# A hybrid RG-LRU and SSD encoder step on one core: TensorE's order in the SSD stage written out by hand

## The chip, the cores and the metric

The kernel runs on one core of one Trainium2 chip. The metric is the device time of one execution in microseconds (us), the median of three runs. The profile is of one more execution of the same program, with a time and a span of its own.

## What is computed

One layer of a streaming encoder is applied to a prompt of 1024 tokens and to a sample of 32 tokens, both 1024 wide. All inputs are fp32. Cut to what matters here:

```python
mod = silu(c) @ w_ada + b_ada
shift, scale, gate = split(mod, 3)
h = rmsnorm(x, norm_g) * (1 + scale) + shift
lru_x, lru_g, xbc, z, dt_raw = split(h @ w_in)        # widths 1024, 1024, 1536, 1024, 16
# RG-LRU group: causal conv of width 4, gates, a scan over time, times silu(lru_g)
# SSD group, 16 heads of 64, 2 groups of B and C, state 128:
xs, B, C = split(silu(causal_conv(xbc)))
dt = softplus(dt_raw + dt_bias); dA = -exp(a_log) * dt
y = ssd_scan(xs * dt, dA, B, C, state) + d * xs        # within a chunk, and from chunk to chunk
y_ssd = grouped_rmsnorm(y * silu(z))
out = x + gate * (concat(y_lru, y_ssd) @ w_out);  y_out = rmsnorm(out, final_norm_g)
```

The new convolution rows and the new states are outputs as well.

## The kernel before, in words

Features lie on the 128 partitions and tokens on the free axis. Prompt and sample share one row of 1060 columns (`TW`): 1024 of the prompt, four of padding, 32 of the sample. The scan works in eight chunks of 128 tokens, and a ninth of the 32 sample tokens.

**Projection in units.** `w_in` is cut into units of 128 output columns. A unit's weights come by one DMA of 512 KB into `wraw` (`fetch_unit`, L96), ScalarE rounds them to `whi` (L101) and VectorE makes the rest `wlo` (L103), with three buffers of each. A unit is then 72 products on TensorE in three blocks of columns: block 2 (290 columns, with two shift columns), block 0 and block 1 (384 each). Each block takes eight times L236, L237, L238 into a PSUM tile `pj`. `pj` tiles have the tag "main" (four PSUM buffers). `shift_bias` (`sb`, L248, VectorE) and `evacuate` (L255, ScalarE) bring a unit to SBUF.

**Everything else on TensorE** in the SSD stage is short fp32 products into PSUM tiles with the tag "g", which are four buffers for all of them. One step of the stage handles one of eight pairs of heads, `j`:

- `ssd_tokens` (L643): nine transposes `xsT` (L652) of the tile `xs`, in three PSUM tiles; VectorE multiplies each into `xw` and `xdt` (L654).
- `ssd_states` (L658): nine products `dS` (L668) in three tiles; VectorE carries the state from chunk to chunk in 16 small instructions (L677).
- `ssd_diag` (L683): 18 products `yd` (L693) with the two decay matrices `M`; VectorE adds them with the skip term into `y` (L696).
- `ssd_off` (L700): eight products `yo` (L708) in three tiles of 384, 512 and 32 columns; VectorE multiplies each by `E` in place (L711), then adds it to `y` (L712). Only the add frees the tile's PSUM buffer.
- `ssd_decay` (L628) prepares the next step's `M` and `E`. SyncE's queue loads the two `M` tiles from `dA_d` in DRAM (L635) and `E` from `E_d` (L631), VectorE scans each `M` (L636), ScalarE takes the exponential (L639), and VectorE masks it with `CBm` (L640). `M` has two buffers, so the loads for step j+1 wait until the `yd` products of step j have read both.
- `gate_row` (L746): a 512 KB unit of `w_ada` and eight products `ada_s` (L120) of 128 columns, then `gate_column` (L750): one product `ada_c` (L127). One unit of the gate for each step.
- `ssd_x` (L754) makes `xs` by the convolution of a projected unit: one ScalarE instruction (L501), three on VectorE (L503), then silu on ScalarE. `ssd_z` and `ssd_gate` (L720) multiply `y` by silu of the z unit.

A step projects two units, x of the next step and z of its own. Once, at j = 4, `group_rstd` adds four products `gs` (L737).

**Ahead of the steps** lie four preparations: `b_post` for B (transposes `bT`, L599), `dt_chain` (a polynomial for softplus on VectorE, some fifty small instructions, then the two products `cs`, L553, and the transposes `dtT`, L570, whose copies go to DRAM as `dA_d` and `E_d` by 18 small DMAs on SyncE's queue, L575 and L576), and `c_post` for C (its convolution, then the products `cb`, L611, which are masked into `CBm`, L615). The units projected there are 27 (C of group 1) and 16 (x of step 0).

**What sets the order.** The start of the kernel is written out by hand for all engines (L313). From L464 on the framework's scheduler orders the instructions of every engine by its own estimate of when they are ready; the program's text gives only the dependences. Each engine takes its instructions strictly in the order that the scheduler has fixed. In the LRU stage that follows, ScalarE's order is by hand again.

Of the kernel before, what the change touches and what calls it, by code (L numbers as in the profile page):

```python
# [16 lines left out]
KT = 8  # L17
# [12 lines left out]
P_NG, P_BADA, P_LCW, P_LCB = 0, 8, 32, 64  # L30
# [33 lines left out]
def encoder_step(ctx: ExitStack, tc: tile.TileContext, a, o):  # L64
# [19 lines left out]
    def pc(base, i=0, n=1):  # L84
        return par[:, base + i:base + i + n]
# [20 lines left out]
    def load_unit(src):  # L106
        return split_unit(fetch_unit(src))
# [8 lines left out]
    def ada_unit(raw, n=1):  # L116
        ps = pbank([128, n * 128], "ada_s")
        for kk in range(KT):
            q = slice(32 * (kk % 4), 32 * (kk % 4) + 32)
            nc.tensor.matmul(ps[q, :], lhsT=sc[:, kk, :], rhs=raw[:, :, kk, :] if n > 1 else raw[:, kk, :],  # L120
                             start=(kk < 4), stop=(kk >= 4))
# [421 lines left out]
    def dt_chain():  # L543
        buf = tw.tile([128, TW], F32, name="dtbuf", tag="y", bufs=1)
        flat = [t.rearrange("p c h -> p (c h)") for t in (dt_tm, w_tm, dtv)]
        softplus(buf, flat[0], flat[2], 144)
        nega = buf[:, 0:16]
        nc.scalar.activation(nega, pc(P_ALOG, 0, 16), AF.Exp)
        nc.vector.tensor_scalar(nega, nega, -1.0, None, op0=OP.mult)
        dA = buf[:, 144:288]  # L550
        nc.vector.tensor_mul(dA.rearrange("p (c h) -> p c h", h=16), dt_tm, nega[:, None, :].to_broadcast([128, 9, 16]))
        ps = pbank([128, 2, 144], "cs")
        nc.tensor.matmul(ps[:, 0, :], lhsT=ge, rhs=dA, start=True, stop=True)  # L553
        nc.tensor.matmul(ps[:, 1, :], lhsT=ones[:, 0:128], rhs=dA, start=True, stop=True)
        Ee = buf[:, 288:432]
        cs = buf[:, 432:576]
        nc.vector.tensor_copy(cs, ps[:, 0, :])
        nc.scalar.activation(Ee, cs, AF.Exp)
        nc.vector.tensor_sub(cs, ps[:, 1, :], cs)
        nc.scalar.activation(cs, cs, AF.Exp)  # L560
        nc.vector.tensor_mul(flat[1], cs, flat[0])
        nc.gpsimd.memset(dec_bc, 0.0)
        nc.scalar.activation(dec_bc[:, 1:8, :].rearrange("p c h -> p (c h)"), ps[:, 1, 16:128], AF.Exp)
        nc.scalar.activation(dec_bc[:, 9, :], ps[:, 1, 128:144], AF.Exp)
        rows = tw.tile([128, TW], F32, name="dtrows", tag="E", bufs=1)
        nc.gpsimd.memset(rows[:, 0:328], 0.0)
        for i, (t, dst) in enumerate(((dA, dA_d), (Ee, E_d))):
            o0 = 164 * i
            pt = pbank([128, 160], "dtT2")
            nc.tensor.transpose(pt[:, 0:128], t[:, 0:128], ident)  # L570
            nc.tensor.transpose(pt[0:16, 128:160], t[0:32, 128:144], ident[0:32, 0:32])
            nc.vector.tensor_copy(rows[:, o0:o0 + 128], pt[:, 0:128])
            nc.vector.tensor_copy(rows[0:16, o0 + 132:o0 + 164], pt[0:16, 128:160])
            for c in range(NCH):
                dma(dst[:, c * 128:(c + 1) * 128], rows[c * 16:(c + 1) * 16, o0:o0 + 128])  # L575
# [25 lines left out]

    def c_post(g, raw):
        u = ssd_conv(raw, 10 + g)
        nc.scalar.activation(CT[:, g, :], u, AF.Silu)
        for cs_ in (range(0, 4), range(4, 8), range(8, 9)):
            n = len(cs_)
            L = chunk_cols(cs_[0])[1]
            pt = pbank([128, n, L], "cb")
            for i, c in enumerate(cs_):
                c0, L = chunk_cols(c)  # L610
                nc.tensor.matmul(pt[0:L, i, :], lhsT=BT[g][:, c0:c0 + L], rhs=CT[:, g, c0:c0 + L],  # L611
                                 start=True, stop=True)
# [4 lines left out]
    b_post(0, raws[0])
    with tc.issue_after(last[0].ins):
        banks = project(load_unit(a["w_in"][27]))
    b_post(1, raws[1])  # L620
    dt_chain()
    c_post(0, raws[2])
    c_post(1, ssd_raw(banks, 11))
# [119 lines left out]

    gate_rows = {}

    def gate_row(k):  # L746
        gate_rows[k] = wpool.tile([128, 128], F32, name="ada_row", tag="ada_row", bufs=2)
        nc.vector.tensor_copy(gate_rows[k], ada_unit(fetch_unit(a["w_ada"][16 + k])))

    def gate_column(k):  # L750
        pcol = ada_columns(gate_rows.pop(k), 1)
        nc.vector.tensor_scalar(gate[:, k, :], pcol[:, 0, :], pc(P_BADA, 16 + k), None, op0=OP.add)

    def ssd_x(j, raw):  # L754
        u = ssd_conv(raw, j)
        nc.scalar.activation(u, u, AF.Silu)
# [6 lines left out]
    with tc.issue_after(last[0].ins):
        xs = ssd_x(0, ssd_raw(project(load_unit(a["w_in"][16])), 0))
        gate_row(0)
    xdt, xw = ssd_tokens(0, xs)
    Ms, E = ssd_decay(0)
    stt = ssd_states(0, xw)
    for j in range(8):
        y = ssd_diag(j, xs, xdt, Ms)  # L770
        wx = load_unit(a["w_in"][17 + j if j < 7 else 0])
        banks = {}
        begin(wx, banks, 2)
        ssd_off(j, y, stt, E)
        banks = project(wx, (2, 0, 1), banks)
        if j < 7:
            Ms, E = ssd_decay(j + 1)
        if j < 7:
            xs = ssd_x(j + 1, ssd_raw(banks, j + 1))
        else:  # L780
            bx = lru_raw(banks, 0)
        wz = load_unit(a["w_in"][28 + j])
        banks = {}
        begin(wz, banks, 2)
        if j == 4:
            group_rstd(0)
        begin(wz, banks, 0)
        gate_column(j)
        if j < 7:
            xdt, xw = ssd_tokens(j + 1, xs)  # L790
        begin(wz, banks, 1)
        zs = ssd_z(banks)
        if j < 7:
            gate_row(j + 1)
            stt = ssd_states(j + 1, xw)
        ssd_gate(j, y, zs)
# [321 lines left out]
```

## Time and profile before

| | |
|---|---|
| median of 3 runs | 766.57 us (766.02 to 767.29) |
| profiled execution | 765.56 us, span 763.8 us |
| TensorE busy | 748.8 us, 98% of the span |
| VectorE busy | 533.6 us, 70% |
| ScalarE busy | 417.9 us, 55% |
| granted TensorE clock, mean | 0.995 |
| SSD stage with its preparations | from 74.2 us (first block of unit 27) to 364.3 us (first block of the LRU stage's first unit) |

The span runs from the first instruction to the last; the execution's own time is 1.8 us longer. "Busy" of TensorE counts each matmul from its issue to its modelled end, and neighbours overlap, so what a product costs is read from the distance between the starts of two rows.

### The profile page before, as it was taken

What the parts mean: (1) busy time and instruction counts of PE and PEld (TensorE: products, weight loads), DVE (VectorE), ACT (ScalarE), POOL (GpSimd) and SP (SyncE); (2) the same over time, 40 slices, a digit from 0 to 9 for tenths busy, and PEclk for the clock granted to TensorE, in tenths of its full rate; (3) what the DMA queues carried; (4) which work ended last, traced back from release to release, by engine and by line L of the source; (5) the groups of instructions that cost most, each with busy time, mean ns of one, the idle gap of its engine ahead of it and who ended that gap; (6) DMA issues with size and microseconds to landing.
All of it is one profiled execution on the core that took longest, in us unless ns stands there. A gap on an engine that the chain in (4) does not pass through costs nothing.

```text
span 763.8 us, 12803 instructions
## 1 busy us (share of the span) xinstructions
PE 748.8 (98%) x5126; PEld 724.4 (95%) x5126; DVE 533.6 (70%) x862; ACT 417.9 (55%) x602; POOL 48.0 (6%) x161
## 2 busy tenths in 40 slices
PE   8999999999999999999999999999999999999994
PEld 7879999999999989999999999999999999999994
DVE  4676969897878768787367556644759897545643
ACT  5565755373543435352776886787777564333330
POOL 1102300010000000000011101100101000000000
PEclk9999999999999999999999999999999999999998
DMA  8852114544343424441321112111244785654831
GB/s 331 314 201 60 56 40 138 156 146 154 111 126 112 124 91 117 151 137 53 83 76 52 58 35 63 29 63 35 60 126 139 222 277 171 199 157 130 272 110 70
DMA packets 40059, 96.31 MB, mean 126 GB/s; under 512 B 4408, under 2 KB 22080, under 8 KB 40000
## 3 DMA queue, kind: packets, MB, share of 16 engines
q1 hardware_dynamic: 40000, 95.49, 39.5%
q8 instruction: 40, 0.66, 0.4%
q14 instruction: 19, 0.16, 0.1%
HBM read 85.53 MB, written 9.95 MB: 125 GB/s over the span
## 4 chain that ended last, share of the span: by engine, by line
PE 88%; DMA 6%; DVE 4%; ACT 1%; issue 1%; SPq 1%; DVEq 0%; ACTq 0%
PE pj L236 15%; PE pj L238 15%; PE pj L237 15%; PE mix L948 8%; PE mix L946 8%; PE mix L947 8%; PE pj L362 4%; PE yd L693 2%; PE dS L668 2%; DMA sraw<-in_w_ada_dram 2%; PE yo L708 1%; DMA wraw<-in_w_in_dram 1%; PE ada_s L120 1%; DMA M<-dA_d 1%; PE xsT L652 1%; PE gt L830 1%
## 5 line engine op out<-in xcount | busy, mean ns | idle before, releaser
L236 PE MATMUL pj<-hb,whi 128*128 128x384 f32 (+1 forms) x792 | 259.4, 328 | 0.0
L238 PE MATMUL pj<-hb,wlo 128*128 128x384 f32 (+1 forms) x792 | 259.0, 327 | 0.0
L237 PE MATMUL pj<-hb,whi 128*128 128x384 f32 (+1 forms) x792 | 258.9, 327 | 0.0
L101 ACT CAST whi<-wraw 128x1024 fp32r<-128x1024 f32 x81 | 84.8, 1047 | 128.5 <-PE mix L947 67.8
L238 PEld LDWEIGHTS pj<-hb,wlo 128*128 128x128 f32 x792 | 149.5, 189 | 1.8 <-issue 1.5
L237 PEld LDWEIGHTS pj<-hb,whi 128*128 128x128 f32 x792 | 149.3, 189 | 1.1 <-issue 0.9
L236 PEld LDWEIGHTS pj<-hb,whi 128*128 128x128 f32 x792 | 148.8, 188 | 1.4 <-issue 1.3
L103 DVE TENSOR_TENSOR wlo<-wraw,whi 128x1024 fp32r<-128x1024 f32 x81 | 98.6, 1219 | 45.6 <-ACT whi L101 45.6
L946 PE MATMUL mix<-yt,whi 128*128 128x324 f32 (+2 forms) x320 | 104.1, 325 | 0.0
L948 PE MATMUL mix<-yt,wlo 128*128 128x324 f32 (+2 forms) x320 | 103.8, 326 | 0.0
L947 PE MATMUL mix<-yt,whi 128*128 128x324 f32 (+2 forms) x320 | 103.7, 324 | 0.0
L503 DVE SCALAR_TENSOR_TENSOR u<-raw,par,u 128x1060 f32<-128x1060 f32 x60 | 78.6, 1312 | 1.5 <-ACT u L501 1.1
L946 PEld LDWEIGHTS mix<-yt,whi 128*128 128x128 f32 x320 | 60.1, 188 | 0.2
L948 PEld LDWEIGHTS mix<-yt,wlo 128*128 128x128 f32 x320 | 60.0, 188 | 0.2
L947 PEld LDWEIGHTS mix<-yt,whi 128*128 128x128 f32 x320 | 60.0, 188 | 0.1
L636 DVE TENSOR_TENSOR_SCAN M<-M,mask 128x1060 f32<-128x1060 f32 x16 | 37.7, 2361 | 10.7 <-DMA M<-dA_d 10.7
L255 ACT ACTIVATE raw<-pj,sb 128x256 f32<-128x256 f32 (+1 forms) x74 | 30.9, 467 | 24.2 <-PE pj L238 20.1
L362 PE MATMUL pj<-hb,whi 128*128 128x384 f32 (+1 forms) x144 | 36.9, 334 | 0.1
L965 DVE SCALAR_TENSOR_TENSOR ot<-mix,gate,xr 128x352 f32<-128x352 f32 (+3 forms) x32 | 14.8, 488 | 25.5 <-PE mix L948 20.9
L639 ACT ACTIVATE M<-M 128x1060 f32<-128x1060 f32 x16 | 17.4, 1090 | 23.9 <-DVE M L636 23.8
L842 DVE SCALAR_TENSOR_TENSOR r<-a,r 128x1060 f32<-128x1060 f32 x8 | 10.1, 1263 | 28.2 <-ACT r L841 28.2
L813 ACT CAST uh<-u 128x1060 fp32r<-128x1060 f32 x8 | 8.6, 1077 | 37.3 <-DVE u L503 37.3
(234 smaller groups left out, 1119.5 us busy)
## 6 DMA issues: line engine op xcount, KB each, us to landing
wraw<-in_w_out_dram SPq DMA_DIRECT2D x48, 512.0 KB, 3.7
wraw<-in_w_in_dram SPq DMA_DIRECT2D x36, 512.0 KB, 3.7
M<-dA_d SPq DMA_DIRECT2D x16, 530.0 KB, 4.5
sraw<-in_w_ada_dram SPq DMA_DIRECT2D x8, 1024.0 KB, 11.9
E<-E_d SPq DMA_DIRECT2D x16, 265.0 KB, 4.3
yz_d<-y SPq DMA_DIRECT2D x8, 530.0 KB, 4.0
wraw<-in_w_ada_dram SPq DMA_DIRECT2D x8, 512.0 KB, 4.9
x<-in_xh_dram SPq DMA_DIRECT2D x4, 384.0 KB, 4.9
```

The source lines that it names most:

```text
L101: nc.scalar.copy(hi, raw)
L103: eng.tensor_sub(lo, raw, hi.bitcast(F32))
L236: nc.tensor.matmul(out, lhsT=hi[:, kk, :], rhs=hh, start=(kk == 0), stop=False)
L237: nc.tensor.matmul(out, lhsT=hi[:, kk, :], rhs=hl, start=False, stop=False)
L238: nc.tensor.matmul(out, lhsT=lo[:, kk, :], rhs=hh, start=False, stop=(kk == KT - 1))
L255: nc.scalar.activation(dst[0:P, off + d:off + d + e - s], banks[b][0:P, s:e], func, bias=sb[0:P, w:w + 1])
L362: nc.tensor.matmul(banks[u][b], lhsT=w[i][:, k, :], rhs=hb[b][:, k, 0 if heads else 1, :], start=(heads and k == 0 and i == 0), stop=(not ...
L503: nc.vector.scalar_tensor_tensor(u, raw[:, k:k + TW], wcol(k), u, op0=OP.mult, op1=OP.add)
L636: nc.vector.tensor_tensor_scan(M, M, mask, 0.0, op0=OP.add, op1=OP.mult)
L946: nc.tensor.matmul(ps, lhsT=w[0][:, k, :], rhs=yh, start=(half == 1 and k == 0), stop=False)
L947: nc.tensor.matmul(ps, lhsT=w[0][:, k, :], rhs=yl, start=False, stop=False)
L948: nc.tensor.matmul(ps, lhsT=w[1][:, k, :], rhs=yh, start=False, stop=(half == 0 and k == KT - 1))
```

## The change

From the end of the hand-written start to the end of the SSD stage, TensorE's instructions now stand in the order of the program's text (`manual_schedule` for TensorE alone). The scheduler still orders VectorE, ScalarE, GpSimdE and SyncE's queue, now around that fixed order. The text is rearranged:

- A unit's blocks are written one by one (`begin`), and each kind of short product is one group between two blocks.
- A step is: `xsT` | blocks 2 and 0 of the next x | `dS` | its block 1 and block 2 of z | `yd` | block 0 of z | `yo` | block 1 of z. Step 0 differs a little: its `xsT` stands after two blocks of unit 17, and only block 1 of z lies between its `yd` and its `yo`.
- In the preparations, unit 16 is begun before `dt_chain`: block 2 of it, the products of `dt_chain`, block 0, `cb` of group 0, block 1, `cb` of group 1. The convolutions of `c_post` become a function of their own, `c_conv`, ahead of block 0.
- The gate's units go in pairs. At even steps one DMA of 1 MB brings two units into a tile `graw`, eight `ada_s` products of 256 columns stand before `xsT`, and two `ada_c` products stand after `yo`, where `group_rstd`'s four also stand at j = 4.

```diff
-    def c_post(g, raw):
+    def c_conv(g, raw):
         u = ssd_conv(raw, 10 + g)
         nc.scalar.activation(CT[:, g, :], u, AF.Silu)
+
+    def c_post(g):
...
     def gate_row(k):
-        gate_rows[k] = wpool.tile([128, 128], F32, name="ada_row", tag="ada_row", bufs=2)
-        nc.vector.tensor_copy(gate_rows[k], ada_unit(fetch_unit(a["w_ada"][16 + k])))
+        raw = tw.tile([128, 2, KT, 128], F32, name="graw", tag="graw", bufs=1)
+        dma(raw, a["w_ada"][16 + k:18 + k].rearrange("i p k n -> p i k n"))
+        gate_rows[k] = wpool.tile([128, 256], F32, name="ada_row", tag="ada_row", bufs=1)
+        nc.vector.tensor_copy(gate_rows[k], ada_unit(raw, 2))
...
+    with tc.manual_schedule(engines={mybir.EngineType.PE}):
+        with tc.issue_after(last[0].ins):
+            w, banks = load_unit(a["w_in"][27]), {}
+        begin(w, banks, 2)
+        begin(w, banks, 0)
+        b_post(0, raws[0])
+        begin(w, banks, 1)
+        raw = ssd_raw(banks, 11)
+        b_post(1, raws[1])
+        with tc.issue_after(last[0].ins):
+            w, banks = load_unit(a["w_in"][16]), {}
+        begin(w, banks, 2)
+        dt_chain()
+        c_conv(0, raws[2])
+        c_conv(1, raw)
+        begin(w, banks, 0)
+        c_post(0)
+        begin(w, banks, 1)
+        c_post(1)
+        xs = ssd_x(0, ssd_raw(banks, 0))
+        Ms, E = ssd_decay(0)
+        for j in range(8):
+            def tokens():
+                if j % 2 == 0:
+                    gate_row(j)
+                return ssd_tokens(j, xs)
+
+            if j:
+                xdt, xw = tokens()
+            wx = load_unit(a["w_in"][17 + j if j < 7 else 0])
+            bx = {}
+            begin(wx, bx, 2)
+            begin(wx, bx, 0)
+            if j:
+                stt = ssd_states(j, xw)
+            else:
+                xdt, xw = tokens()
+            begin(wx, bx, 1)
...
+            wz = load_unit(a["w_in"][28 + j])
+            banks = {}
+            begin(wz, banks, 2)
+            if j:
+                y = ssd_diag(j, xs, xdt, Ms)
+            else:
+                stt = ssd_states(j, xw)
+            begin(wz, banks, 0)
+            if j == 0:
+                y = ssd_diag(j, xs, xdt, Ms)
+                begin(wz, banks, 1)
+            ssd_off(j, y, stt, E)
+            if j < 7:
+                xs = ssd_x(j + 1, raw)
+                Ms, E = ssd_decay(j + 1)
+            if j % 2 == 0:
+                gate_column(j)
+            if j == 4:
+                group_rstd(0)
+            if j:
+                begin(wz, banks, 1)
+            ssd_gate(j, y, ssd_z(banks))
```

The lines of the moved functions shift by six: what was L652 to L712 is L646 to L706 in the new kernel, and L636 and L640 are L630 and L634. In the diff the branches on `j` are the places where step 0 differs.

**TensorE at `dt_chain`.** First as it stood. `pj_1303` is block 2 of unit 17, so unit 16 lies wholly ahead of these rows.

```order
L238 MATMUL pj_1303<-hb_85,wlo 128x290
L236 MATMUL pj_1303<-hb_85,whi 128x290
L553 MATMUL cs<-dtbuf,ge 128x144
L554 MATMUL cs<-dtbuf,ones 128x144
L570 MATMUL dtT_983<-ident,dtbuf 128x128
L571 MATMUL dtT_983<-ident,dtbuf 16x32
L237 MATMUL pj_1303<-hb_85,whi 128x290
```

And now; `pj_964` is block 2 of unit 16 and `pj_1097` its block 0.

```order
L238 MATMUL pj_964<-hb_85,wlo 128x290
L553 MATMUL cs<-dtbuf,ge 128x144
L554 MATMUL cs<-dtbuf,ones 128x144
L570 MATMUL dtT_1029<-ident,dtbuf 128x128
L571 MATMUL dtT_1029<-ident,dtbuf 16x32
L570 MATMUL dtT_1043<-ident,dtbuf 128x128
L571 MATMUL dtT_1043<-ident,dtbuf 16x32
L236 MATMUL pj_1097<-hb_83,whi 128x384
```

The products of `dt_chain` have moved forward past blocks 0 and 1 of unit 16 and most of block 2 of unit 17.

**VectorE after `yd`, in step 6.** As it stood, from the two halves of `yd` on: `yo`'s products followed `yd`'s at once, and their multiplications and adds stand before and between the two scans.

```order
L696 SCALAR_TENSOR_TENSOR y<-u,par,yd 128x512
L696 SCALAR_TENSOR_TENSOR y<-u,par,yd 128x32
L711 TENSOR_TENSOR yo<-yo,E 128x384
L712 TENSOR_TENSOR y<-y,yo 128x384
L711 TENSOR_TENSOR yo<-yo,E 128x512
L636 SCALAR_TENSOR_TENSOR M<-M,mask 128x1060
L712 TENSOR_TENSOR y<-y,yo 128x512
L711 TENSOR_TENSOR yo<-yo,E 128x32
L103 TENSOR_TENSOR wlo<-wraw,whi 128x1024
L636 SCALAR_TENSOR_TENSOR M<-M,mask 128x1060
L712 TENSOR_TENSOR y<-y,yo 128x32
```

And now:

```order
L503 SCALAR_TENSOR_TENSOR u<-raw,par,u 128x1060
L630 SCALAR_TENSOR_TENSOR M<-M,mask 128x1060 x2
L705 TENSOR_TENSOR yo<-yo,E 128x384
L705 TENSOR_TENSOR yo<-yo,E 128x512
L634 TENSOR_TENSOR M<-M,CBm 128x1060
L705 TENSOR_TENSOR yo<-yo,E 128x32
L706 TENSOR_TENSOR y<-y,yo 128x384
L749 TENSOR_TENSOR gate<-ada_c,par 128x4
L706 TENSOR_TENSOR y<-y,yo 128x512
L634 TENSOR_TENSOR M<-M,CBm 128x1060
L706 TENSOR_TENSOR y<-y,yo 128x32
```

Both scans, and two masks, have moved ahead of the adds. Steps 1 to 6 differ from this only in whether a mask stands one place earlier or later; step 0 has a `wlo` after the first `yo` row. In the built program the three `xsT` tiles of a step take PSUM buffers that the step before gives up last: in steps 2, 4 and 6 those of `yo`'s three tiles, in the odd steps those of `yo`'s two large tiles and of `ada_c` (in step 5, of `ada_c`, `gs` and `yo`'s tile of 512). So `xsT` waits for these adds.

**TensorE at j = 4**, where `pj_2657` is block 0 and `pj_2731` block 1 of that step's z. Before, `gs` stood between two blocks, a whole unit away from `yo`; now:

```order
L238 MATMUL pj_2657<-hb_83,wlo 128x384
L702 MATMUL yo<-CT,dS 128x128 x7
L702 MATMUL yo<-CT,dS 128x32
L127 MATMUL ada_c<-sel,ada_row 128x2 x2
L731 MATMUL gs<-ssq,ones 32x265 x4
L236 MATMUL pj_2731<-hb_84,whi 128x384
```

The tile of `gs` takes the PSUM buffer of the first `yo` tile, so it waits for the add of 384 columns.

More of the change, by code (lines that the diff above doesn't have):

```diff
@@ L615, in c_post @@
             nc.vector.tensor_mul(dst, pt[0:L], ge[0:L, None, 0:L].to_broadcast([L, n, L]))
[L617 to L623, printed above, removed]
     ssqs = {}
@@ L746, in gate_row @@
     def gate_row(k):
-        gate_rows[k] = wpool.tile([128, 128], F32, name="ada_row", tag="ada_row", bufs=2)
-        nc.vector.tensor_copy(gate_rows[k], ada_unit(fetch_unit(a["w_ada"][16 + k])))
+        raw = tw.tile([128, 2, KT, 128], F32, name="graw", tag="graw", bufs=1)
+        dma(raw, a["w_ada"][16 + k:18 + k].rearrange("i p k n -> p i k n"))
+        gate_rows[k] = wpool.tile([128, 256], F32, name="ada_row", tag="ada_row", bufs=1)
+        nc.vector.tensor_copy(gate_rows[k], ada_unit(raw, 2))
     def gate_column(k):
-        pcol = ada_columns(gate_rows.pop(k), 1)
-        nc.vector.tensor_scalar(gate[:, k, :], pcol[:, 0, :], pc(P_BADA, 16 + k), None, op0=OP.add)
+        pcol = ada_columns(gate_rows.pop(k), 2)
+        nc.vector.tensor_add(gate[:, k:k + 2, :], pcol, pc(P_BADA, 16 + k, 2)[:, :, None].to_broadcast([128, 2, 2]))
     def ssd_x(j, raw):
@@ L761, in begin @@
         mm_block(banks[b], w, b)
[L763 to L796, printed above, removed]
+    with tc.manual_schedule(engines={mybir.EngineType.PE}):
[36 more added lines that the diff above has]
+            if j < 7:
+                raw = ssd_raw(bx, j + 1)
+            else:
+                bx = lru_raw(bx, 0)
+            wz = load_unit(a["w_in"][28 + j])
[3 more added lines that the diff above has]
+                y = ssd_diag(j, xs, xdt, Ms)
+            else:
+                stt = ssd_states(j, xw)
[4 more added lines that the diff above has]
+            ssd_off(j, y, stt, E)
+            if j < 7:
+                xs = ssd_x(j + 1, raw)
[7 more added lines that the diff above has]
+            ssd_gate(j, y, ssd_z(banks))
```

## The prediction

> **What bounds the kernel now.** I read the page's first part, then the sums by stage, then TensorE's timeline through one late step, then VectorE's beside it. TensorE first:
>
> ```profile
> span 763.8 us, 12803 instructions
> PE 748.8 (98%) x5126; PEld 724.4 (95%) x5126; DVE 533.6 (70%) x862; ACT 417.9 (55%) x602; POOL 48.0 (6%) x161
> ```
>
> ```profile
> 300.00:340.00 40.00, 40.00 (x309) 38.22 (x308) 31.76 (x54) 17.19 (x24) 1.10 (x10) 1.00 0.34 106
> ```
>
> In the SSD stage TensorE has work in all of 40 us, VectorE in 31.8, and the granted clock is full. So the time is TensorE's: what the change takes off its work is gained, and every microsecond for which it has to wait is lost. A step in TensorE's timeline (starts; "x" counts two records for an fp32 product, one for a transpose):
>
> ```profile
> 303.83 1.15 PE L652 MATMUL xsT<-ident,u 128*128 128x128 f32 x9
> 304.90 0.65 PE L120 MATMUL ada_s<-wraw,sc 128*32 128x128 f32 x16
> 305.48 0.44 PE L238 MATMUL pj<-hb,wlo 128*128 128x384 f32 x1
> ...
> 309.64 2.36 PE L668 MATMUL dS<-xw,B_tm 128*128 128x128 f32 x18
> 311.93 1.09 PE L693 MATMUL yd<-M,xdt 128*64 128x128 f32 x16
> 312.95 0.44 PE L237 MATMUL pj<-hb,whi 128*128 128x384 f32 x1
> ...
> 316.14 1.33 PE L693 MATMUL yd<-M,xdt 128*64 128x128 f32 x20
> 317.40 1.83 PE L708 MATMUL yo<-CT,dS 128*128 128x128 f32 x14
> 318.99 0.43 PE L236 MATMUL pj<-hb,whi 128*128 128x384 f32 x1
> ```
>
> Prices from the starts: 23 products between 305.48 and 309.64, so a block of 384 costs 4.25. `xsT` costs 1.1, `dS` 2.3, `yd` 1.02 + 1.26 = 2.3, `yo` 1.6 and its last product 0.1, one unit's `ada_s` 0.58. The first block product after a short group takes 0.1 to 0.2 more than its neighbours.
>
> VectorE and SyncE's queue at the same place; in square brackets the idle time ahead and what ended it:
>
> ```profile
> 317.29 0.91 DVE L696 SCALAR_TENSOR_TENSOR y<-u,par,yd 128x512 f32<-128x512 f32 x2 [2.32 <-PE yd L693]
> 318.38 0.57 DVE L711 TENSOR_TENSOR yo<-yo,E 128x384 f32<-128x384 f32 x1 [0.18 <-PE yo L708]
> 318.98 0.55 DVE L712 TENSOR_TENSOR y<-y,yo 128x384 f32<-128x384 f32 x1
> 319.45 0.69 DVE L711 TENSOR_TENSOR yo<-yo,E 128x512 f32<-128x512 f32 x1
> 321.67 2.37 DVE L636 TENSOR_TENSOR_SCAN M<-M,mask 128x1060 f32<-128x1060 f32 x1 [1.52 <-DMA M<-dA_d]
> 323.95 0.66 DVE L712 TENSOR_TENSOR y<-y,yo 128x512 f32<-128x512 f32 x1
> 324.53 0.19 DVE L711 TENSOR_TENSOR yo<-yo,E 128x32 f32<-128x32 f32 x1
> 325.76 2.36 DVE L636 TENSOR_TENSOR_SCAN M<-M,mask 128x1060 f32<-128x1060 f32 x1
> 328.04 0.16 DVE L712 TENSOR_TENSOR y<-y,yo 128x32 f32<-128x32 f32 x1
> 328.12 1.25 DVE L640 TENSOR_TENSOR M<-M,CBm 128x1060 f32<-128x1060 f32 x1
> ```
>
> ```profile
> 317.50 0.80 SPq L635 DMA_DIRECT2D M<-dA_d  x2
> ```
>
> The loads of `M` go out when `yd` ends (317.40), and 4.2 us later the scan starts. While VectorE waits those 1.52 us, the add of 512 columns that stands behind the scan waits too, though its inputs are there. Today this costs nothing: the next `xsT` is 16 us away.
>
> **What the change saves.** The step's short groups returned to a block 63 times (counted in TensorE's timeline from 74.2 to 364.3 us), in the new order 37 times: 26 x 0.09 = 2.3 less, of which about 0.7 goes back because eight `dS` groups no longer run straight into `yd`. For the gate in pairs:
>
> ```profile
> 21.29 1.07 PE L120 MATMUL ada_s<-sraw,sc 128*32 128x256 f32 x16 [0.53 <-DMA sraw<-in_w_ada_dram]
> ```
>
> A pair's `ada_s` takes 1.0 against 2 x 0.58; with `ada_c` about 0.2 a pair, 0.8 in all. Sum: **2.4 saved**, from 1 (if returns get dearer) to 5 (if small waits go too). The gate's bytes stay the same; one 1 MB load in two steps replaces two of 512 KB and has over 50 us.
>
> **Wait A, at the products of `dt_chain`: 8.3.**
>
> ```profile
> 87.88 0.38 PE L236 MATMUL pj<-hb,whi 128*128 128x290 f32 x1
> 91.19 0.34 PE L236 MATMUL pj<-hb,whi 128*128 128x384 f32 x1
> 102.24 0.41 PE L553 MATMUL cs<-dtbuf,ge 128*128 128x144 f32 x2
> ...
> 108.76 2.23 PE L611 MATMUL cb<-CT,bt 128*128 128x128 f32 x18
> ```
>
> ```profile
> 99.02 0.17 DVE L549 TENSOR_SCALAR dtbuf<-dtbuf 128x16 f32<-128x16 f32 x1 [0.82 <-ACT dtbuf L548]
> 99.23 0.31 DVE L551 TENSOR_TENSOR dtbuf<-dt_tm,dtbuf 128x144 f32<-128x144 f32 x1
> ```
>
> Block 2 of unit 16 ends at 91.19, and what is ahead of it on all engines has not changed. `cs` now stands there, and its input is L551's, which ends at 99.54. The cover that is gone is the 11 us of block products up to 102.24. All of TensorE's queue stands behind `cs`.
>
> **Wait B, at step 0's `xsT`: 4.7.** After `cs` come the transposes, of which the second waits for an exponential (to 101.1), block 0 (105.4), `cb` (2.2, to 107.6), block 1 (112.0), `cb` (114.0), unit 17's blocks 2 and 0 (121.6) and `ada_s` (122.6). `xs` is later:
>
> ```profile
> 107.85 1.09 ACT L756 ACTIVATE u<-u 128x1060 f32<-128x1060 f32 x1
> ```
>
> ```profile
> 102.62 1.32 DVE L503 SCALAR_TENSOR_TENSOR u<-raw,par,u 128x1060 f32<-128x1060 f32 x1 [0.62 <-ACT u L501]
> ```
>
> ```profile
> 104.43 3.58 SPq L575 DMA_DIRECT2D dA_d<-dtrows  x8
> 109.19 3.55 SPq L575 DMA_DIRECT2D E_d<-dtrows  x8
> 113.30 1.99 SPq L635 DMA_DIRECT2D M<-dA_d  x2
> ```
>
> The 18 small DMAs occupy SyncE's queue for 8 us from 100.8, then the first `M` loads: VectorE's scan starts at 113.0. Behind it in VectorE's order stand two `CBm`, a `wlo`, a mask (to 118.9), a convolution pass of 1.25, the second scan (to 122.4), two passes and a mask (to 126.1); silu on ScalarE ends at 127.3.
>
> **Wait C, at step 1's `xsT`: 7.5.** From 127.3, step 0 adds 1.0 + 4.3 + 3.3 + 2.4 + 4.3 + 2.3: `yd` ends at 144.9. TensorE then has one block, `yo` and `ada_c`, until 151.3. VectorE has, from 149.1: two scans 4.6, `yo` 384 0.6, `wlo` 1.1, `yo` 512 and 32 0.7, add 384 0.5, mask, gate and mask 2.5, add 512 0.6: 159.7. `xsT` can't have its buffers before the adds and ends at 159.9 instead of 152.4.
>
> **The steps after it.** Count from `yd`'s end. TensorE: block 4.4, `yo` 6.1, block 10.5; after an odd step `ada_s` 11.5, after an even one `ada_c` and so 10.7. VectorE: scans 4.2 to 8.7, `yo` 384 9.3, `yo` 512 9.9, mask 11.1, `yo` 32 11.2, add 384 11.7, add 512 12.3, mask 13.5, add 32 13.6. `xsT` in an even step needs all three adds and ends at 13.8, not 12.5: 1.3 lost, three times. In an odd one it needs the adds of 384 and 512: 1.1 lost, twice (steps 3 and 7). At j = 4 **wait D**: `gs` is ready to run at 6.4 and needs the add of 384 at 11.8: 5.4, after which step 5's `xsT` is free.
>
> Waits: 8.3 + 4.7 + 7.5 + 3.9 + 2.2 + 5.4 = **32.0**. The steps' share hangs on when `M` lands:
>
> ```profile
> DMA to landing us min/median/max: 4.0/4.5/5.5
> ```
>
> At the latest landing each of six steps and wait C would lose 1.3 more, 9 in all; the other end is that the steps after C lose nothing.
>
> **The clock.** Such waits can also cost clock:
>
> ```profile
> 0.00:5.00 5.00, 3.84 (x18) 3.85 (x19) 0.63 (x3) 2.45 (x3) 2.76 (x15) 1.00 0.50 143
> 5.00:10.00 5.00, 5.00 (x44) 5.00 (x44) 1.92 (x2) 3.68 (x6) 0.00 (x0) 1.00 1.02 368
> ```
>
> ```profile
> 752.00:754.00 2.00, 0.36 (x3) 0.10 (x1) 1.00 (x3) 0.47 (x1) 0.00 (x0) 1.00 0.00 0
> ...
> 756.00:758.00 2.00, 0.40 (x4) 0.25 (x3) 1.57 (x4) 0.00 (x0) 0.00 (x0) 0.66 0.00 0
> ```
>
> The dense work ends at 752.4. A mean of 0.66 over two microseconds that end at 0.5 means a drop at 756.6: 4.3 us later. At the start 18 matmuls take 213 ns each, after it 114, so coming back costs about 3.84 us at half pace, 1.9 lost. C and D pass 4.3: 1.9 each. A passes too, but B's wait, set by VectorE and SyncE, hides about half: 1.0. Sum **4.8**.
>
> The Trainium skill's page "TensorE: Matmul & The Clock Gate", section "Part 1: The HAM clock gate", puts the window at about 3.4 us of idleness, and as much busy time to come back; by it B counts too. This speaks against an order that leaves TensorE waiting, beyond the wait itself. The rows show 4.3 and 3.84, and I use those.
>
> **Sum.** 765.56 - 2.4 + 32.0 + 4.8 = 800.0 for the profiled execution. The median of the runs before lies 1.0 above its profiled execution, so **801**.
>
> **The rivals.**
> - Clock rivals. By the idle window above the clock falls in all four waits at full price: 4 x 1.9 = 7.6, 804 (0.17). The page named above states that rule. Or it never falls: 796 (0.18); for it speaks that the clock is still full from 752 to 754, with 0.36 us of work.
> - Only the preparations wait: in the steps VectorE and DMA come earlier than I count, A to C remain: 20.5 - 2.4 + 2.9, so 788 (0.15). Against it: 4.2 us from `yd` to scan in the rows, and scans ahead of adds in the order.
> - Faster: the fewer returns decide, at all the short groups, because the polynomial in `dt_chain` is done when TensorE gets to `cs` and the adds when it gets to `xsT`. It gives 764 (0.03), and decides if the waits together stay under 2.4, so `cs` would have to start by 93.6. Against it stands L551 at 99.23, for which nothing of the change is a help.
> - Little change: waits that happen to equal the savings (0.02).
>
> **How the numbers follow.** My forecast has 0.45, and with both clock rivals 0.80. The range goes from 787 (steps that wait for nothing) to 810 (loads of `M` at their latest). Faster by over 0.2% has 0.03, within 0.2% 0.02, slower 0.95; 0.2% is 1.5 us and about what a measurement of this kernel can tell from no change (the three runs differ by 1.27).
>
> **What would show it.** In the new profile: TensorE idle ahead of `cs` from about 91 to 99.5, released by VectorE's `dtbuf`; idle ahead of steps 0's and 1's `xsT` and of `gs`, all but the first released by VectorE's adds to `y` (step 0's by ScalarE's silu); `yd` to `yd` 33 us and more in the steps; PEclk below 9 after the long waits. I am wrong if `cs` doesn't wait, or if in the steps the adds stand done when `xsT` comes.

## The result, and the profile after

| | before | after |
|---|---|---|
| median | 766.57 us (5 runs, 765.87 to 768.74) | 801.14 us (5 runs, 800.80 to 804.49) |
| profiled execution | 765.56 us | 804.49 us |
| SSD stage with its preparations | 290.1 us | 327.2 us, from 76.37 to 403.59 |

The ratio is 1.0458, 95% interval 1.0439 to 1.0477: slower by 34.6 us; a median of 801 (787 to 810) was forecast. The profiled execution lies 3.4 above its median; its mean clock is 0.970, that of the other four 0.973 to 0.974. Against the profiled execution before it is 38.9 longer: 37.1 of this is in the stage, and 1.7 in a window of half clock ahead of it, at 55.6 to 59.1 us.

The first part of the page, TensorE's row: busy 759.2 us of a longer span, 95% where it had been 98%.

```profile
span 802.8 us, 12627 instructions
PE 759.2 (95%) x5062; PEld 733.8 (91%) x5062; DVE 532.6 (66%) x854; ACT 417.9 (52%) x600; POOL 46.9 (6%) x161
PEclk9999978979999999999999999999999999999998
```

VectorE does the same work as before (532.6 against 533.6). What is new is TensorE's waiting, and a clock below 9 in slices 6, 7 and 9. What TensorE waited for in the changed kernel (us in total, times, longest), the waits in the SSD stage only:

```profile
PE xsT L646 <- DVE y L706: 8.8, 6, 6.3
PE cs L553 <- DVE sp16n L582: 8.3, 1, 8.3
PE gs L731 <- DVE gate L749: 5.0, 1, 5.0
PE xsT L646 <- ACT u L753: 3.7, 1, 3.7
...
PE xsT L646 <- DVE gate L749: 2.2, 2, 1.4
...
PE dtT L570 <- ACT dtbuf L558: 0.4, 1, 0.4
```

28.4 us in all. The releaser that the profile names is the VectorE instruction that came last: `sp16n` stands two places behind L551 and `gate` one place behind the add of 384, which are what the products need. These two end at 101.70 and at 299.28, and `cs` and `gs` start 0.15 us later:

```profile
101.39 0.31 DVE L551 TENSOR_TENSOR dtbuf<-dt_tm,dtbuf 128x144 f32<-128x144 f32 x1
...
298.74 0.54 DVE L706 TENSOR_TENSOR y<-y,yo 128x384 f32<-128x384 f32 x1
```

The four long waits in TensorE's timeline, with the idle time ahead in brackets (the run of `xsT` below it is the same step's last tile):

```profile
101.85 0.82 PE L553 MATMUL cs<-dtbuf,ge 128*128 128x144 f32 x2 [8.35 <-DVE sp16n L582]
...
132.20 2.18 PE L646 MATMUL xsT<-ident,u 128*128 128x128 f32 x9 [3.66 <-ACT u L753]
...
164.94 2.27 PE L646 MATMUL xsT<-ident,u 128*128 128x128 f32 x8 [6.29 <-DVE y L706]
167.86 0.40 PE L646 MATMUL xsT<-ident,u 128*32 128x128 f32 x1 [0.65 <-DVE y L706]
...
299.43 1.11 PE L731 MATMUL gs<-ssq,ones 128*32 128x265 f32 x8 [4.98 <-DVE gate L749]
```

At wait B, TensorE ends its `ada_s` at 128.5, and silu of step 0's `xs` on ScalarE ends at 132.15:

```profile
127.47 1.07 PE L120 MATMUL ada_s<-graw,sc 128*32 128x256 f32 x16
...
131.06 1.09 ACT L753 ACTIVATE u<-u 128x1060 f32<-128x1060 f32 x1 [0.25 <-DVE u L503]
```

VectorE at wait C shows the mechanism: the scans wait for `M`'s load, and the multiplications and adds of `yo`, whose first tile TensorE had ended at 157.2, stand behind them. `xsT` starts when the add of 384 is done, and its last tile after the add of 512, which has the two masks ahead of it as well.

```profile
157.43 4.62 DVE L630 TENSOR_TENSOR_SCAN M<-M,mask 128x1060 f32<-128x1060 f32 x2 [4.62 <-DMA M<-dA_d]
161.97 0.54 DVE L705 TENSOR_TENSOR yo<-yo,E 128x384 f32<-128x384 f32 x1
...
163.55 0.79 DVE L705 TENSOR_TENSOR yo<-yo,E 128x512 f32<-128x512 f32 x2
164.25 0.54 DVE L706 TENSOR_TENSOR y<-y,yo 128x384 f32<-128x384 f32 x1
164.71 1.25 DVE L634 TENSOR_TENSOR M<-M,CBm 128x1060 f32<-128x1060 f32 x1
...
165.96 1.25 DVE L634 TENSOR_TENSOR M<-M,CBm 128x1060 f32<-128x1060 f32 x1
167.13 0.77 DVE L706 TENSOR_TENSOR y<-y,yo 128x512 f32<-128x512 f32 x2
```

The clock behind the waits, in a table of windows (PEclk is the third column from the end, in front of DMA share and GB/s): 0.50 behind A, behind B, behind C and around `gs`.

```profile
104.00:108.00 4.00, 4.00 (x13) 3.71 (x14) 0.78 (x4) 0.55 (x3) 0.10 (x1) 0.50 0.08 18
...
134.00:137.00 3.00, 3.00 (x11) 3.00 (x10) 2.23 (x6) 0.00 (x0) 0.00 (x0) 0.50 0.00 0
...
168.00:171.00 3.00, 3.00 (x14) 3.00 (x14) 3.00 (x5) 0.00 (x0) 0.00 (x0) 0.50 0.24 65
298.00:304.00 6.00, 4.58 (x19) 3.76 (x20) 4.94 (x9) 1.47 (x2) 0.00 (x0) 0.50 0.35 90
```

**How the stage is summed below.** From the starts in TensorE's timeline I take how long each group lasts, and set against it what a group of its kind lasts where it waits for nothing (a block of 384 4.34 us, `xsT` 0.90, and so on). The sum of what is over, "excess", is 42.0 us in the changed kernel: 28.4 of waits, 12.4 of half clock (TensorE works for 8.0, 5.4, 6.1 and 5.4 us in the four slow stretches, and half of that is lost), 1.2 in small gaps. Without it the stage would last 285.2 us, 4.9 less than before.

### The profile page after: what moved, and what is told of

Same layout as the page of the kernel before. It is cut to its first block, busy times and chain, and to the rows that moved or that the text cites. A ratio compares the mean times of both kernels' runs of the same rounds, so it can differ in the third digit from the quotient of the medians.

```text
span 802.8 us, 12627 instructions
## 1 busy us (share of the span) xinstructions
PE 759.2 (95%) x5062; PEld 733.8 (91%) x5062; DVE 532.6 (66%) x854; ACT 417.9 (52%) x600; POOL 46.9 (6%) x161
## 4 chain that ended last, share of the span: by engine, by line
PE 80%; DVE 10%; DMA 7%; issue 1%; ACT 1%; SPq 0%; DVEq 0%; ACTq 0%
PE pj L236 14%; PE pj L237 14%; PE pj L238 14%; PE mix L977 8%; PE mix L975 8%; PE mix L976 8%; DMA M<-dA_d 4%; PE pj L362 4%; DVE M L630 4%; PE dS L662 2%; PE yd L687 2%; DVE M L634 2%; DMA sraw<-in_w_ada_dram 2%; DMA wraw<-in_w_in_dram 1%; DVE yo L705 1%
## 5 line engine op out<-in xcount | busy, mean ns | idle before, releaser
L236 PE MATMUL pj<-hb,whi 128*128 128x384 f32 (+1 forms) x792 | 264.6, 334 | 0.0
L237 PE MATMUL pj<-hb,whi 128*128 128x384 f32 (+1 forms) x792 | 260.5, 329 | 0.0
L236 PEld LDWEIGHTS pj<-hb,whi 128*128 128x128 f32 x792 | 151.7, 192 | 2.9 <-issue 1.3
L237 PEld LDWEIGHTS pj<-hb,whi 128*128 128x128 f32 x792 | 152.2, 192 | 0.0
L238 PEld LDWEIGHTS pj<-hb,wlo 128*128 128x128 f32 x792 | 152.1, 192 | 0.0
L103 DVE TENSOR_TENSOR wlo<-wraw,whi 128x1024 fp32r<-128x1024 f32 x81 | 98.6, 1219 | 59.4 <-ACT whi L101 59.4
L630 DVE TENSOR_TENSOR_SCAN M<-M,mask 128x1060 f32<-128x1060 f32 x16 | 37.1, 2354 | 15.6 <-DMA M<-dA_d 15.6
L671 DVE SCALAR_TENSOR_TENSOR dS<-dS,dec_bc 128x64 f32<-128x64 f32 x128 | 25.7, 275 | 17.7 <-ACT dS L666 17.7
L362 PE MATMUL pj<-hb,whi 128*128 128x384 f32 (+1 forms) x144 | 37.3, 336 | 0.1
L871 DVE SCALAR_TENSOR_TENSOR r<-a,r 128x1060 f32<-128x1060 f32 x8 | 10.1, 1263 | 28.2 <-ACT r L870 28.2
```

Of the source, the lines that this page charges most:

```text
L103: eng.tensor_sub(lo, raw, hi.bitcast(F32))
L236: nc.tensor.matmul(out, lhsT=hi[:, kk, :], rhs=hh, start=(kk == 0), stop=False)
L237: nc.tensor.matmul(out, lhsT=hi[:, kk, :], rhs=hl, start=False, stop=False)
L238: nc.tensor.matmul(out, lhsT=lo[:, kk, :], rhs=hh, start=False, stop=(kk == KT - 1))
L362: nc.tensor.matmul(banks[u][b], lhsT=w[i][:, k, :], rhs=hb[b][:, k, 0 if heads else 1, :], start=(heads and k == 0 and i == 0), stop=(not ...
L630: nc.vector.tensor_tensor_scan(M, M, mask, 0.0, op0=OP.add, op1=OP.mult)
```

## Experiments

The theory on trial: every long wait is an order on VectorE or ScalarE that TensorE now meets too early, plus the clock that the waits cost. The rivals: VectorE is simply too full; the clock isn't the waits' doing; the groups or the pairs cost something themselves. All kernels are edits of the changed kernel, unless it is said otherwise. "Stage" is from the first block of unit 27 to the first block of the LRU stage; excess is given where the written order and its products are those of the change or nearly so. Each ratio is to runs of the kernel before that were made beside that run (median 766.41 for e1 to e4, 767.67 for e5 to e8, 767.79 for e9 and e10), so medians of different groups compare to about 1.4 us only.

| run | median us | ratio to before (95%) | stage us | excess us |
|---|---|---|---|---|
| changed kernel | 801.14 | 1.0458 (1.0439 to 1.0477) | 327.2 | 42.0 |
| e1_prep | 794.94 | 1.0359 (1.0331 to 1.0387) | 320.2 | 36.3 |
| e2_gs_early | 802.22 | 1.0455 (1.0411 to 1.0499) | 323.2 | 38.0 |
| e3_adds_first | 785.65 | 1.0233 (1.0195 to 1.0271) | 308.7 | 23.5 |
| e4_fill | 796.04 | 1.0379 (1.0352 to 1.0405) | 319.0 | |
| e5_dve_prep | 793.78 | 1.0358 (1.0324 to 1.0392) | 315.9 | 30.6 |
| e6_no_waits | 773.92 | 1.0088 (1.0064 to 1.0112) | 295.3 | 10.1 |
| e7_r1 | 781.01 | 1.0186 (1.0168 to 1.0204) | 305.3 | 20.0 |
| e8_pairs | 768.65 | 1.0026 (1.0006 to 1.0046) | 289.9 | |
| e9_best | 763.88 | 0.9945 (0.9933 to 0.9958) | 287.6 | 2.3 |
| e10_returns | 769.09 | 1.0014 (1.0000 to 1.0027) | 291.4 | |

### e3: the adds ahead of the scans

```diff
-                Ms, E = ssd_decay(j + 1)
+                with tc.issue_after(added.ins):      # the last add of ssd_off
+                    Ms, E = ssd_decay(j + 1)
```

> The changed kernel (801.1), with the scans and masks of the next step's M held behind the last of yo's adds in VectorE's order. TensorE's order is the same. Theory (C, D and the losses in the steps come from adds that stand behind scans, which wait for M's load): xsT of step 1 waits 1 to 2 us instead of 6.3, gs waits 1 us instead of 5.0, the other steps' xsT wait for nothing, and the half clock behind C and D goes: 11 less in waits in C and D, 6 in the steps, 4 of clock, so about 781, from 778 to 785. A and B stay as they are. Rival (VectorE is simply full there, and what is moved ahead of a scan is only paid at the next yd, which needs M): the wait moves to yd or dS, and the time stays within 3 us of 801.

The stage is 18.5 us shorter. TensorE's waits in this kernel:

```profile
PE cs L553 <- DVE sp16n L582: 8.3, 1, 8.3
PE xsT L646 <- ACT u L754: 3.6, 1, 3.6
...
PE pj L236 <- ACT zs L255: 2.0, 1, 2.0
...
PE xsT L646 <- DVE y L706: 0.9, 1, 0.9
```

C is down to 0.9, D and the losses of the steps are gone: from one step's `yd` to the next's it is 32.0, 31.3 and 32.0 us from step 1 to step 4, where the changed kernel has 33.2, 32.4 and 33.1. `M`, now later, makes nobody wait. So C, D and the steps are the order of scans and adds, not VectorE's load, which is the same. The time misses 781, and a new wait of 2.0 in step 5, with 1.6 of half clock behind it, accounts for 3.6 of it: z's evacuation is late there.

### e7: a buffer for the square root's tile

```diff
-        r1 = cpool.tile([128, n], F32, name="r1", tag="zs", bufs=1)
+        r1 = (cpool if g else tw).tile([128, n], F32, name="r1", tag="r1" if not g else "zs", bufs=1)
```

> e3_adds_first (785.65) with a buffer of its own for the tile that group_rstd's square root writes. Theory (the one wait that e3 shows in step 5, 2.1 us inside block 2 and 1.6 of slow clock behind it, is z's evacuation waiting until that tile has gone out by its DMA): 782, from 781 to 783. Rival (block 2 waits for something else): 785 to 786.

The stage is 3.4 us shorter than e3's and the time 781.0. The changed kernel already had this dependence (`r1` has the buffer of `zs`, and must go out by a DMA first): ScalarE waits 3.60 us there, until 304.68, but TensorE, held back by D, doesn't wait for it.

### e2: `gs` ahead of `yo`

```diff
+            if j == 4:
+                group_rstd(0)
             ssd_off(j, y, stt, E)
...
-            if j == 4:
-                group_rstd(0)
```

> The changed kernel (801.1), with group_rstd's four products ahead of step 4's yo instead of behind its ada_c. Nothing else is changed. Theory (gs waits only because the PSUM buffer it gets is that of yo's first tile, which the add of 384 frees): gs then has a free buffer and starts at once, the 5.0 us of wait D and the 2.5 us at half clock behind it go, and step 5's xsT then waits for the adds as in the other odd steps, 1.0 to 1.4: about 795, from 793.5 to 796.5. Rival (ssq itself is late, or the wait only moves to the next xsT at full size): 799 to 801.

A miss. `gs` does start at once, but `ada_c` now waits, and from step 4's `yd` to step 5's it is 38.8 us instead of 39.5:

```profile
289.20 0.66 PE L731 MATMUL gs<-ssq,ones 128*32 128x265 f32 x8
289.79 1.97 PE L702 MATMUL yo<-CT,dS 128*128 128x128 f32 x16
295.46 1.01 PE L127 MATMUL ada_c<-sel,ada_row 128*128 128x2 f32 x4 [3.71 <-ACT r L734]
```

The four "g" buffers go round in the written order, so the fourth tile behind `gs` gets its buffer, and only ScalarE's square root frees that. ScalarE has it behind the first exponential of `M`, which waits for the scan, and a table load:

```profile
291.24 1.28 ACT L633 ACT_TABLE_LOAD   x1 [2.31 <-DVE M L630]
...
293.63 1.28 ACT L734 ACT_TABLE_LOAD   x1
294.93 0.48 ACT L734 ACTIVATE r<-gs,eps 128x265 f32<-128x265 f32 x1
```

So the rival held in a form that I hadn't thought of: the wait moves to `ada_c`, and what it hangs on is again the scans. The stage's 4.0 are spread over slow stretches and waits that came out shorter, and 0.7 of them are at this place; the time can't be told from that of the changed kernel.

### e4: TensorE kept busy in the waits

```diff
+    def fill(w, banks, b, n):
+        banks[b] = pbank([128, BLK[b][1]], f"pj{b}", tag="main")
+        for i in range(n):
+            nc.tensor.matmul(banks[b], lhsT=w[0][:, i % KT, :], rhs=hb[b][:, i % KT, 0, :], start=True, stop=True)
...
+        fill(w, banks, 0, 44)
         dt_chain()
...
+                fill(wx, bx, 1, 34)
                 xdt, xw = tokens()
```

> The changed kernel (801.1), with products of no use put where TensorE waits, so that it is busy there: 44 of 384 columns ahead of cs, 34 of 384 ahead of step 0's ada_s, 44 of 290 ahead of step 1's xsT, 26 of 384 ahead of gs. They write into the PSUM tile that the next block overwrites, and are shorter than the waits. Theory (idleness in a wait costs clock behind it): the granted clock stays full, a block of 384 behind cs takes 4.2 instead of 6.9, one behind step 0's xsT 4.2 instead of 5.9. A's part is hidden, since what A's blocks gain B waits longer; B, C and D give back 2.5 to 2.8 each: about 793, from 791 to 796. Rival 1 (the clock fell only behind A, C and D as forecast, 1.9 each): 796 to 797. Rival 2 (the slow stretches behind the waits are not due to idleness): 800 to 803. One mask of 1.25 us stands ahead of step 0's add of 384 in VectorE's order here, which can give 1.2 back.

The clock is full everywhere in the stage; these are the windows of the blocks that ran at 0.50 before, behind A and behind B:

```profile
104.00:108.00 4.00, 4.00 (x24) 3.96 (x24) 0.59 (x3) 0.55 (x3) 0.10 (x1) 1.00 0.09 19
132.00:137.00 5.00, 5.00 (x33) 4.99 (x32) 2.95 (x7) 0.17 (x1) 0.00 (x0) 1.00 0.63 213
```

In 4 us TensorE begins 24 products instead of 13. The stage is 8.2 us shorter with 148 products more. The median gains 5.1 (the changed kernel's profiled execution lies 3.4 above its median, this one's 1.0). So the slow stretches come from the idleness, and by these two numbers the clock cost 5 to 8 us of the time, all four waits together (less than the 12.4 lost in them, since part of what is lost behind A would have been waited at B). B's share excludes the rival in which its wait was too short to count.

### e1 and e5: the preparations, in TensorE's order and in VectorE's

e1 moves TensorE's products (and, in the text, x's convolution ahead of C's), e5 leaves them and moves VectorE's:

```diff
 e1:     begin(w, banks, 2)
-        dt_chain()
-        c_conv(0, raws[2])
-        c_conv(1, raw)
         begin(w, banks, 0)
-        c_post(0)
         begin(w, banks, 1)
+        dt_chain()
+        xs = ssd_x(0, ssd_raw(banks, 0))
+        c_conv(0, raws[2])
+        c_conv(1, raw)
...
+        begin(wx, bx, 2)
+        c_post(0)
+        begin(wx, bx, 0)
         c_post(1)
-        xs = ssd_x(0, ssd_raw(banks, 0))
         Ms, E = ssd_decay(0)
...
 e5:
-        dt_chain()
-        c_conv(0, raws[2])
-        c_conv(1, raw)
+        cs_copy = dt_chain()
+        with tc.issue_after(cs_copy.ins):
+            c_conv(0, raws[2])
+            c_conv(1, raw)
...
-        Ms, E = ssd_decay(0)
+        with tc.issue_after(last_pass[0].ins):      # the last pass of xs's convolution
+            Ms, E = ssd_decay(0)
```

> The changed kernel (801.1), with the preparations in another written order: all three blocks of unit 16 ahead of the products of dt_chain, unit 17's block 2 and the first cb behind them, then block 0 and the second cb. Nothing else is changed. Theory (A and B are waits on VectorE's chain, met because TensorE stands there too early): cs starts without a wait at 99 to 100 us on the time base of the profile before, xsT of step 0 comes about 16 us earlier than after the change, and the wait A (8.5), the wait B (3.7) and the half clock behind both (about 6) go: 782 to 787. Rival 1 (VectorE's load sets when step 0's xs is ready, wherever TensorE's products stand): the wait at cs goes, but the wait at xsT grows by as much: 797 to 802. Rival 2 (my own terms, with 1.0 us of clock for A and none for B): 787 to 789.

> The changed kernel (801.1) with TensorE's written order untouched and another order on VectorE in the preparations: the convolutions of C stand behind dt_chain's copy of cs, and the two scans of step 0's M behind the convolution of step 0's xs. Theory (A and B are VectorE passes that stand ahead of what TensorE waits for): cs starts without a wait of over 0.5 us after unit 16's block 2, cb has its CT, step 0's xsT waits under 1 us, no slow clock in the preparations; the 16 us between the end of that block and the end of step 0's xsT that are not products go: 785, from 783 to 788. Rival (as in the first of these runs: C's convolutions, now later, make cb wait, and what cs gains cb loses): 793 to 796. Waits C, D and the steps stay as they are.

Both theories miss; e1 lies between its theory and its rival, and e5 comes out as its rival said (793 to 796). In e1 `cs` waits for nothing, but `cb` does, for C's convolutions, which the scheduler has put behind `dt_chain` and x's, and step 0's `xsT` still waits 2.0:

```profile
113.84 4.03 PE L613 MATMUL cb<-CT,bt 128*128 128x128 f32 x18 [6.50 <-ACT CT L604]
```

In e5 the wait B is gone and `xsT` of step 0 ends at 123.9 instead of 134.0 (1.7 of that is an earlier start of the stage), but `cs` still waits and so does `cb`:

```profile
93.72 0.64 PE L555 MATMUL cs<-dtbuf,ge 128*128 128x144 f32 x2 [1.92 <-DVE dtbuf L553]
...
105.77 2.23 PE L616 MATMUL cb<-CT,bt 128*128 128x128 f32 x18 [3.07 <-ACT CT L607]
```

VectorE has `dt_chain`, C's convolutions and x's one after another, and whichever comes last holds up its own product. Each of the two edits moved one engine to fit the other's old order, and uncovered the next wait: what a wait lasts isn't what taking it away alone gives back. In e1 x's convolution changed its place too, so which of the two moves made `cb` wait is not told apart.

### e6: e3, e5 and e7 together

> The order on VectorE of e5_dve_prep and of e3_adds_first together, and a buffer of its own for the tile that group_rstd's square root writes (it shared one with silu of z). TensorE's written order is that of the changed kernel. Theory (the waits were the whole loss, and the order saves 2.4 when it waits for nothing): the kernel before minus 2.4, so 764, from 763 to 766, TensorE without a wait of over 1 us in the stage. Rival 1 (what e3 and e5 gain overlaps, or other waits appear): 768 to 775. Rival 2 (the groups save nothing): 766 to 767, no faster than the kernel before.

773.9, in the rival's range: excess 10.1, of which 8.6 in the preparations as in e5. The steps lose nothing after step 1's `xsT`. The excess taken off, the stage is 285.3 again: with and without waits the products of the new order take 4.8 to 4.9 less than the stage before, twice what I had forecast.

### e9: a written order made to wait for nothing

```diff
         begin(w, banks, 2)
-        dt_chain()
         c_conv(0, raws[2])
-        c_conv(1, raw)
         begin(w, banks, 0)
+        c_conv(1, raw)
         c_post(0)
+        wx = load_unit(a["w_in"][17])
+        bx = {}
         begin(w, banks, 1)
+        dt_chain()
+        xs = ssd_x(0, ssd_raw(banks, 0))
+        begin(wx, bx, 2)
         c_post(1)
-        xs = ssd_x(0, ssd_raw(banks, 0))
-        Ms, E = ssd_decay(0)
+        begin(wx, bx, 0)
...
+                xdt, xw = tokens()
+                with tc.issue_after(last_xdt[0].ins):
+                    Ms, E = ssd_decay(0)
```

> e6_no_waits with the preparations rewritten so that TensorE comes to each product when its input is there: unit 16's block 2, its block 0, cb of group 0, its block 1, then the products of dt_chain, unit 17's block 2, cb of group 1, unit 17's block 0; C's convolutions ahead of dt_chain in the text, and the scans of step 0's M behind its xdt. The steps are those of e6_no_waits. Theory (e6's stage lasts 295.3 us, of which 10.1 are waits and half clock, and 8.6 of these are in the preparations): the stage lasts about 287, 3 less than the 290.1 of the kernel before; time 763.5, from 762 to 766. Rival (M of step 0, whose path now starts later, makes its yd wait by 2 to 6 us): 766 to 771.

763.88, ratio 0.9945 (0.9933 to 0.9958): faster than the kernel before, and by 37 us than the changed one, whose groups it keeps. Its stage lasts 287.6 against 290.1, 2.5 less; the profiled executions, 763.97 against 765.56, differ by 1.6. It has the steps of e6, so it holds the edits of e3 and e7 as well, and in the stage TensorE still waits 0.9 at the second `dtT` and 0.9 at step 1's `xsT`. The page's first part, for comparison with the rows above:

```profile
span 762.3 us, 12631 instructions
PE 746.3 (98%) x5062; PEld 724.9 (95%) x5062; DVE 531.7 (70%) x854; ACT 423.0 (55%) x606; POOL 47.4 (6%) x161
PEclk9999999999999999999999999999999999999997
```

### e10: 28 returns more

```diff
+    def parts(w, banks, b):
+        def between(i):
...
+            for kk in ((0, 1, 2), (3, 4, 5), (6, 7))[i]:
+                mm_part(banks[b], w, b, kk)
...
+                stt = ssd_states(j, xw, parts(wx, bx, 1))
...
+                y = ssd_diag(j, xs, xdt, Ms, parts(wz, banks, 0))
```

> e9_best with 28 more returns from short products to a block: in steps 1 to 7 the three tiles of dS stand in three pieces between nine, nine and six products of the x unit's block 1, and the three of yd likewise in block 0 of z. The same products, in another order. My price of a return (0.09 us): the stage is 2.5 us longer than that of e9_best. The other price (0.15, which e6's blocks give against those of the kernel before: 4.0 us less for 26 returns less): 4.2 longer. Rival (returns cost nothing, and the 4.0 were small waits in the kernel before): within 0.5.

The stage is 3.75 longer than e9's: 0.134 us a return, nearer to 0.15 than to my 0.09. A piece of `yd` in this kernel:

```profile
195.75 0.33 PE L238 MATMUL pj<-hb,wlo 128*128 128x384 f32 x1
196.01 1.09 PE L691 MATMUL yd<-M,xdt 128*64 128x128 f32 x16
197.03 0.45 PE L236 MATMUL pj<-hb,whi 128*128 128x384 f32 x1
197.32 0.34 PE L237 MATMUL pj<-hb,whi 128*128 128x384 f32 x1
```

Within a block a product starts 0.18 after the last. Coming back it takes 0.29, which I had counted, and going out to `yd` 0.26, which I hadn't. Going out to `dS` costs nothing: there the next product starts 0.18 after the last, the median of all such places. Half of the 28 returns pay for both ways, and half for one.

### e8: the kernel before with the gate in pairs

```diff
+        if j % 2 == 0:
+            gate_column(j)
...
+            if j % 2:
+                gate_row(j + 1)
```

(`gate_row` and `gate_column` as in the change.)

> The kernel before, with the gate's units in pairs as in the change and nothing else. Theory (0.2 a pair): 0.8 less, 765.6, from 764.5 to 766.6, hardly to be told from no change by the time; in the trace a pair's ada_s 1.0 us where two single ones took 1.15. Rival (the load of 1 MB or its tile makes the next unit's weights late): a wait ahead of a block or of ada_s, 768 and more.

The stage is 0.2 shorter and shows no new wait. The time, 768.65 over 12 runs from 765.89 to 774.8, has an interval that lies 0.06% to 0.46% above the kernel before, and is in the rival's range (768 and more). The rival's wait isn't in the stage. Far behind it, at 609.1 us, TensorE waits 1.64 us for a `wlo`, which it doesn't in the profile of the kernel before; whether the pairs bring that about, no run shows. The pairs were worth 0.2 in the stage, not 0.8.

## Why the prediction was right

| term | forecast | measured |
|---|---|---|
| wait A | 8.3 | 8.35, and 0.39 at the second `dtT` |
| wait B | 4.7 | 3.66 |
| wait C | 7.5 | 6.29 + 0.65 |
| wait D | 5.4 | 4.98 |
| steps 2, 4, 6; 3 and 7 | 3.9; 2.2 | 8.8 - 6.94 = 1.9; 2.2 |
| all waits | 32.0 | 28.4 |
| clock | 4.8 | 12.4 in the profiled execution |
| saved | 2.4 | 4.9 |
| small gaps | | 1.2 |
| net | +34.4 | +37.1 in the stage |

The waits stand at the places, and hang on the instructions, that the prediction named, and e3, e4, e7 and e9 show the causes by taking them away. That the total fits to 0.2 us is luck: waits and savings came out 3.6 and 2.5 us better than forecast, the clock 7.6 worse and the small gaps 1.2. The profiled execution, forecast at 800.0, took 804.49; and the forecast added 1.0 to it for the median, where the median lies 3.35 below it (its clock of 0.970 against 0.974, over 803 us, is 3.2 of that). The waits and their places were not luck.

- **Waits A to D and the steps.** Right within 1.1 us each but for the even steps, where the idle time that the profile counts is half of the forecast; by the groups' lengths they lose 1.1 to 1.2 each, and the rest is among the small gaps. B is shorter than forecast since the half clock behind A brought TensorE there 3.7 later, `xs` only 2.7 later.
- **The clock is the step that failed.** I had the clock fall 4.3 us after dense work ends, so B didn't count, and 1.9 for coming back. It fell behind B too (0.50 from 134 to 137), and TensorE worked 5.4 to 8.0 us at half pace each time, 2.7 to 4.0 lost. That is the rival with all four waits, at a higher price than I gave it there. The page "TensorE: Matmul & The Clock Gate" of the Trainium skill, section "Part 1: The HAM clock gate", has a window of about 3.4 us that runs freely. By it B's 3.7 us can count, and this case's traces agree with the length: in each of them the changes of the clock record lie whole multiples of 3.41 us apart. That the window is one of idleness, as the prediction takes it from the Trainium skill, they don't bear out, and the traces decide: TensorE was busy for 36% of the window that ended in the drop at B, 127.32 to 130.74. The 4.3 that I took from the end of the program was the rest of one window and the whole of the next, 753.21 to 756.62.
- **The savings.** 26 returns at 0.134 are 3.5, where I had 2.3 less 0.7; the gate 0.2 for 0.8. Of the 4.9 some 1.2 remains that no run takes apart.
- **The rival in which only the preparations wait** fell (with the losses of C, D and the steps taken away, the stage is 18.5 shorter in e3 and 21.9 in e7), and the time of the one in which the fewer returns decide is what e9 reaches: it needed the waits gone, not the change undone.

## What to carry to other kernels

A written order on one engine fixes where that engine asks for its inputs, and the scheduler then orders the others around it; so for each short group look up when its input is there and when its buffer is freed, on the engine that delivers them, before fixing its place. Price a wait with the work that it hides and the clock behind it, and expect that a wait taken away alone uncovers the next. Grouping was worth it here (0.134 us a return), but 26 returns pay for one wait of 3.5 us.

## What the runs showed of the hardware

**A wait's length doesn't decide over the clock.** In e6 TensorE waits 1.92 us at `cs` and the clock halves; then 3.07 us at `cb`, and it stays full. One-microsecond windows of e6 (PE busy first, PEclk third from the end):

```profile
93.00:94.00 1.00, 0.00 (x0) 0.00 (x0) 0.00 (x0) 0.99 (x2) 0.00 (x0) 1.00 0.93 365
94.00:95.00 1.00, 0.09 (x1) 0.12 (x1) 0.68 (x6) 0.70 (x3) 0.00 (x0) 0.97 0.22 86
95.00:96.00 1.00, 1.00 (x5) 0.96 (x5) 0.00 (x0) 0.16 (x1) 0.36 (x2) 0.50 0.00 0
...
104.00:105.00 1.00, 0.00 (x0) 0.00 (x0) 0.93 (x1) 0.98 (x2) 0.00 (x0) 1.00 0.08 18
105.00:106.00 1.00, 0.00 (x0) 0.00 (x0) 0.00 (x0) 0.99 (x2) 0.26 (x3) 1.00 0.09 20
106.00:107.00 1.00, 0.03 (x1) 0.03 (x1) 0.00 (x0) 1.00 (x2) 0.00 (x0) 1.00 0.12 28
```

The clock record changes at 94.94 and 101.77, two windows of 3.41 apart. The first wait lies within the window that ends at 94.94, in which TensorE is busy 44% of the time; the second is cut in two by a boundary at 105.19 (62% and 48%). In the SSD stage of the changed kernel and of e1 to e7 all 19 such windows at full clock with TensorE busy 44% or less (by its records) were followed by half clock; of nine with 46% to 62% two were. A wait of 2 us may thus cost 3 us more (at `cs`, two windows at half clock with TensorE busy 88% and 100%) or nothing, by where it falls in a window. That this is why executions of the same kernel with waits differ is likely, but no run here shows it.

**A window of half clock without a wait.** In 8 of the 12 profiled executions the clock is at half for one window of 3.41 us between 53.9 and 59.4 us, with TensorE busy all the time, which loses 1.7 us, and the stage starts at 75.9 us or later. The profiles of the kernel before, e5, e8 and e9 haven't got it, and their stages start at 74.2 to 74.9. What sets it off stays open.
